# One level of Strassen-Winograd in the q/k/v projection of a dilated-attention layer, with the layout, buffers and evacuations that it needs

## The chip, the cores and the metric

The kernel runs on all 8 cores of one Trainium2 chip, one sequence of the batch on each core; nothing is exchanged between cores. The metric is the device time of the slowest core in microseconds (us). A program on 8 cores has a slower state here: the cores of one die (0 to 3 or 4 to 7), sometimes of both, get a lower TensorE clock in some executions.

## The reference, cut to what matters

A trunk of two layers: an mLSTM mixer, then a mixture of three dilated sliding-window attentions, each layer followed by a gated ConvFFN. The change touches the attention mixer:

```python
D_MODEL = 2048; BATCH = 8; SEQ = 2048
A_HEAD_DIM = 128; A_HEADS = 16
A_GROUPS = ((128, 1), (512, 4), (2048, 16))     # (window, dilation)

def dilated_mixer(h, positions, w_in, w_out):
    proj = (h @ w_in).astype(jnp.float32).reshape(B, S, A_N_GROUPS, 3, A_HEADS, A_HEAD_DIM)
    for g, (window, dilation) in enumerate(A_GROUPS):
        q = partial_rope(proj[:, :, g, 0], positions)      # rope on 32 of 128 channels
        k = partial_rope(proj[:, :, g, 1], positions)
        o, lse = dilated_band_attention(q, k, proj[:, :, g, 2], window, dilation)
        ...
    alpha = jax.nn.softmax(jnp.stack(lses), axis=0)
    o = jnp.sum(alpha[..., None] * jnp.stack(outs), axis=0)
    return o.reshape(B, S, A_WIDTH).astype(h.dtype) @ w_out
```

For a core this is, 48 times (16 heads x 3 groups), a product of 2048 tokens x 2048 features x 384 columns (128 each of q, k, v), a banded attention, and a sum over the three groups of numerators and denominators.

## The kernel before

Each engine has its own instruction stream. A recording layer tracks who wrote and read which 256-byte page of SBUF and which PSUM bank, and sets the semaphore waits. The attention stage walks over 768 units of 128 tokens. In a unit, TensorE makes the projection in one accumulation of 16 matmuls; the tokens are the stationary operand, the 384 weight columns the moving one:

```python
    def P(n):
        idx, u = divmod(n, 16)
        ...
        for kc in range(16):
            R.mm(PS[:, bk, 0:384], c.hT[:, kc, ts_], W[:, kc, :], kc == 0, kc == 15)
        R.act(QKV[:, n % 16, :], PS[:, bk, 0:384], AF.Copy)               # ScalarE
        R.copy("dve", Rr[(n // 4) % 2][:, n % 4], ...)                    # VectorE, rope channels
```

`ts_` takes every first, fourth or sixteenth token, by the group's dilation. Some units later follow, for four units at a time, rope on GpSimd (`rope`) and the transposes of q and k (`Tr`), and for pairs of units scores, exp and mask (`Sm`) and the products with v and with ones (`AV`). In the third group the pair is finished, with columns 16 apart:

```python
            vN, vD = v3(accN[:]), v3(accD[:])
            R.tt("dve", vD, p3(pD), vD, ALU.add)
            R.recip(vD, vD)                                               # VectorE
            R.tt("dve", vN, p3(pN), vN, ALU.add)
            R.tt("pool", v3(c.yT[:, h, :]), vN, vD, ALU.mult)             # GpSimd
```

Then the output projection (`phase_out`) multiplies `yT` by its weights. At the start of the stage the norm of the last quarter of the tokens (`c.pend`, made by `second`) is still under way and is worked off beside the first units.

The softmax here doesn't subtract the row's maximum and nothing guards it: scores larger than these inputs give would overflow.

Of the kernel before, what the change touches and what calls it, by code (L numbers as in the profile page):

```python
# [19 lines left out]
PAGE = 256  # L20
# [274 lines left out]
def unit_tokens(g):  # L295
    d = ATT_GROUPS[g][1]
    nb = S // d // 128
    tok = np.zeros((16, 128), dtype=np.int64)
    for r in range(d):
        for n in range(nb):  # L300
            tok[r * nb + n] = r + d * (128 * n + np.arange(128))
    return tok
# [75 lines left out]
def build_program():  # L378
# [10 lines left out]
    T["rope"] = nc.dram_tensor("rope", [128, 2, 768], F32, kind="Internal").ap()  # L389
    T["wdb"] = nc.dram_tensor("wdb", [2, 16, 4, 128, 11, 128], BF16, kind="Internal").ap()  # L390
# [32 lines left out]
    c.B = R.sb("B", [128, 7, 8, 512], F16, c.HA)  # L423
    c.yT = R.sb("yT", [128, 16, S], BF16, c.R1)
# [490 lines left out]
class out_weights:  # L915
# [9 lines left out]
    def load(self):  # L925
        if self.n < 16:
            self.c.R.dma("pool", self.w[self.n][:], self.c.T["m_wo" if self.l == 0 else "a_wo"][self.n], f"ow{self.n}")
            self.n += 1
# [17 lines left out]
def norm_tiles(c, li, src, tq, rstd, xr, xcnt, out_dram=None):  # L946
# [14 lines left out]
    for fc in range(ahead):  # L961
        ld(fc)
    for fc in range(16):
        if fc + ahead < 16:
            ld(fc + ahead)
        x = xr[(base + fc) % len(xr)]
        R.stt(x[:], x[:], gvec[:, fc:fc + 1], rstd, ALU.mult, ALU.mult)
        if shv is not None:
            up = li in (2, 3)
            R.act(quarter(c, tq, fc) if up else c.hT[:, fc, sl], x[:], AF.Identity, bias=shv[:, fc:fc + 1])  # L970
            if up and tq % 2 == 1 and fc >= 8:
                combine(c, fc - 8)
        else:
            c.final.append(R.dma("sp", T["outT"][:, fc, sl], x[:], f"st_o{(base + fc) % len(xr)}", dw=[("out", fc, tq)]))
        yield
    xcnt[0] = base + 16

def phase_out(c, l):
# [17 lines left out]
    while W.n < 16:  # L996
        W.load()
# [10 lines left out]
    for tb in range(2):  # L1008
        for fo in range(16):
            for sub in range(2):  # L1010
# [17 lines left out]
                m += 1  # L1028
                if tb == 1 and fo >= (1, 4)[l]:
                    bg = pull(bg, 1 + (m % (4, 2)[l] == 0))  # L1030
# [97 lines left out]
def phase_ffn(c, l):  # L1128
# [106 lines left out]
    for tb in range(2):  # L1235
# [17 lines left out]
        for n_, (fo, ss) in enumerate(order):  # L1253
# [30 lines left out]
            if tb == 1:  # L1284
                if fo == 15:
                    drain(bg)
                    s_ = ss[0]
                    bg = final_norm(c, acc[s_], rst, xk, s_) if last else second(c, li, dst, 2 + s_, acc[s_], rst, nx)
# [8 lines left out]
def second(c, li, src, tq, acc, rst, xr):  # L1297
    rstd_of(c, acc[:], rst[:], 7)
    yield
    yield from norm_tiles(c, li, src, tq, rst[:], xr, [0])  # L1300
# [14 lines left out]
def phase_attn(c):  # L1315
    R, T, PS = c.R, c.T, c.PS
    o = c.R2
    wa = c.att_w
    cur = [o]
    lim = [o + kb(24)]  # L1320

    def t(name, shape, dt_, n=1):
# [5 lines left out]
        for i in range(n):  # L1328
            if lim[0] < c.END and cur[0] + b > lim[0]:
                cur[0], lim[0] = o + kb(48), c.END  # L1330
            r.append(R.sb(f"a_{name}{i}", shape, dt_, cur[0]))
            cur[0] += b
        assert cur[0] <= lim[0], (name, cur[0], lim[0])
        return r if n > 1 else r[0]
    QKV = t("qkv", [128, 16, 384], BF16)
    qkT = t("qkT", [128, 2, 16, 128], BF16)
    PT = t("PT", [128, 4, 128], BF16, 2)
    Rr = t("R", [128, 4, 2, 32], F32, 2)
    cs = t("cs", [128, 2, 48, 16], F32)
    tA = t("tA", [128, 2, 4, 16], F32)  # L1340
    tB = t("tB", [128, 2, 4, 16], F32)
    t("pad", [128, 256], F32)
    accD = t("accD", [128, S], F32)
    accN = t("accN", [128, S], F32)
    mask = t("mask", [128, 4, 128], BF16)
    mrow = t("mrow", [128, 128], F32)
    bg = c.pend
    c.pend = None
    wab = [R.sb(f"a_wab{i}", [128, 16, 128], BF16, c.R1 + kb(56 + 4 * i)) for i in range(2)]
    LO, HI, EVERY, FIRST = 128, 192, 8, 20  # L1350

    def ada_load(i):
        if i < HI:
            R.dma("pool", wab[i % 2][:], T["w_ada"][i], f"wab{i % 2}")
    ada_load(LO)
    ada_load(LO + 1)
    R.dma("sp", cs[:].rearrange("p a b c -> p (a b c)"), T["rope"].rearrange("p a b -> p (a b)"), "ropel", dr=["rope"])
    for i in range(4):
        R.copy("pool", mask[:, i, :], c.tri[:] if i < 2 else c.tri_ge[:])
    seq = [(h, g) for h in range(16) for g in range(3)]  # L1360
    NU = len(seq) * 16

    def utok(g, u):
        d = ATT_GROUPS[g][1]
        nb = S // d // 128
        r, n = u // nb, u % nb
        st = r + d * 128 * n
        return slice(st, st + d * 127 + 1, d) if d > 1 else slice(st, st + 128)

    def P(n):  # L1370
        idx, u = divmod(n, 16)
        h, g = seq[idx]
        if u == 0 and idx + 1 < len(seq) and idx > 0:
            c.att_load(idx + 1)
        W = wa[idx % 2]
        bk = n % 2
        ts_ = utok(g, u)
        for kc in range(16):
            R.mm(PS[:, bk, 0:384], c.hT[:, kc, ts_], W[:, kc, :], kc == 0, kc == 15)
        ct, part = LO + (n - FIRST) // EVERY, (n - FIRST) % EVERY  # L1380
        here = n >= FIRST and ct < HI
        if here and part == 0:
            ada_rows(c, ct, wab[ct % 2], mrow, PS[:, bk, 384:512])
        if here and part == 1:
            ada_sum(c, ct, mrow, PS[:, bk, 384:385])
        R.act(QKV[:, n % 16, :], PS[:, bk, 0:384], AF.Copy)
        R.copy("dve", Rr[(n // 4) % 2][:, n % 4], PS[:, bk, 0:256].rearrange("p (a d) -> p a d", a=2)[:, :, 0:32])
        if here and part == 0:
            R.act(mrow[:], PS[:, bk, 384:512], AF.Copy)
            ada_load(ct + 2)  # L1390
        if here and part == 1:
            R.tt("dve", c.modT[:, ct:ct + 1], PS[:, bk, 384:385], c.badaT[:, ct:ct + 1], ALU.add)
            gm_after(c, ct)

    def rope(j):
        g = seq[j // 4][1]
        u0 = (j % 4) * 4
        s0 = (j % 4) * 4
# [4 lines left out]
        q = QKV[:, s0:s0 + 4, 0:256].rearrange("p u (a d) -> p a u d", a=2)  # L1403
# [7 lines left out]
    def Tr(j, qk):  # L1411
        s0 = (j % 4) * 4
        for i in range(4):
            R.mm(PS[:, 2 + qk, i * 128:(i + 1) * 128], QKV[:, s0 + i, qk * 128:(qk + 1) * 128], c.identb[:], True, True)
        out = qkT[:, qk, s0:s0 + 4, :]
        in_ = PS[:, 2 + qk, :].rearrange("p (u s) -> p u s", u=4)
        if qk == 0:
            R.copy("dve", out, in_)
        else:
            R.act(out, in_, AF.Copy)  # L1420

    def pair(m):
        idx, j = divmod(m, 8)
        h, g = seq[idx]
        nb = S // ATT_GROUPS[g][1] // 128
        a, b = 2 * j, 2 * j + 1
        return idx, j, h, g, a, b, a % nb > 0, b % nb > 0

    def Sm(m):
        idx, j, h, g, a, b, pa, pb = pair(m)  # L1430
        bk = 4 + m % 2
        sl = lambda u: u % 16
        R.mm(PS[:, bk, 0:128], qkT[:, 1, sl(a), :], qkT[:, 0, sl(a), :], True, True)
        R.mm(PS[:, bk, 128:256], qkT[:, 1, sl(b), :], qkT[:, 0, sl(b), :], True, True)
        n = 2
        if pb:
            R.mm(PS[:, bk, 256:384], qkT[:, 1, sl(b - 1), :], qkT[:, 0, sl(b), :], True, True)
            n = 3
        if pa:
            R.mm(PS[:, bk, 384:512], qkT[:, 1, sl(a - 1), :], qkT[:, 0, sl(a), :], True, True)  # L1440
            n = 4
        pt = PT[m % 2]
        R.act(pt[:, 0:n, :], PS[:, bk, 0:n * 128].rearrange("p (a s) -> p a s", a=n), AF.Exp, scale=128.0 ** -0.5)
        R.tt("dve", pt[:, 0:n, :], pt[:, 0:n, :], mask[:, 0:n, :], ALU.mult)

    def AV(m):
        idx, j, h, g, a, b, pa, pb = pair(m)
        bk = 6 + m % 2
        pt = PT[m % 2]
        V = lambda u: QKV[:, u % 16, 256:384]  # L1450
        R.mm(PS[:, bk, 0:128], V(a), pt[:, 0, :], True, not pa)
        if pa:
            R.mm(PS[:, bk, 0:128], V(a - 1), pt[:, 3, :], False, True)
        R.mm(PS[:, bk, 128:256], V(b), pt[:, 1, :], True, not pb)
        if pb:
            R.mm(PS[:, bk, 128:256], V(b - 1), pt[:, 2, :], False, True)
        if not pa:
            R.mm(PS[:, bk, 256:384], c.onesb[:], pt[:, 0, :], True, True)
            R.mm(PS[:, bk, 384:512], c.onesb[:], pt[:, 1, :], True, not pb)
            if pb:  # L1460
                R.mm(PS[:, bk, 384:512], c.onesb[:], pt[:, 2, :], False, True)
        else:
            R.mm(PS[:, bk, 256:384], c.onesb[:], pt[:, 0, :], True, False)
            R.mm(PS[:, bk, 256:384], c.onesb[:], pt[:, 3, :], False, True)
            R.mm(PS[:, bk, 384:512], c.onesb[:], pt[:, 1, :], True, False)
            R.mm(PS[:, bk, 384:512], c.onesb[:], pt[:, 2, :], False, True)
        pN, pD = PS[:, bk, 0:256], PS[:, bk, 256:512]
        if g == 0:
            R.copy("dve", accN[:, j * 256:(j + 1) * 256], pN)
            R.copy("dve", accD[:, j * 256:(j + 1) * 256], pD)  # L1470
        elif g == 1:
            st = j // 2 + 512 * ((j % 2) * 2)
            vN, vD = accN[:, st:st + 1021:4], accD[:, st:st + 1021:4]
            R.tt("dve", vN, pN, vN, ALU.add)
            R.tt("dve", vD, pD, vD, ALU.add)
        else:
            r0 = 2 * j
# [70 lines left out]
```

## Time and profile before

| | before |
|---|---|
| first four executions | 7414.49, 7443.39, 7601.44, 8290.82 us |
| profiled execution | 7443.39 us; cores 7396.2 to 7441.9 |
| attention stage, first to last projection matmul | 2367 us, a third of the whole |
| TensorE busy, granted clock in its body | 99%, 1.00 |

The profile is a page with the busy time of each engine, the chain of work that ended last, and groups of equal instructions ("line engine op out<-in shapes xcount | busy us, mean ns of one | idle time before them, and who ended it"). Rows of stretches give the busy time of TensorE, its weight loads, VectorE (DVE), ScalarE (ACT) and GpSimd (POOL) in a window, then granted clock, DMA share and GB/s. Rows in order of time give start, duration and instruction; for a run of matmuls the duration is that of the whole run. Matmuls are pipelined, so their cost is the distance of their starts, not their duration.

### The profile page before, as it was taken

Reading aid. Unit: us, or ns where it says so; the run is one execution under the profiler, and the core shown is the slowest. Engines: PE = TensorE matmul, PEld = TensorE weight load, DVE = VectorE, ACT = ScalarE, POOL = GpSimd, SP = SyncE. Lnnn points to the kernel's source line nnn. Section 1 sums busy time; section 2 is a strip of 40 time slices with the busy share of each in tenths; the row PEclk is TensorE's granted clock in tenths of the full one; section 3 lists DMA queues with packets and bytes.
Section 4 is the critical chain, followed back from the end, with each engine's and each line's share of the span. In section 5 each row is a group of like instructions: output and inputs, shape, how many; then the busy total and the mean of one; then the engine's idle time right before and its main releaser. Section 6 shows DMA issues by size and latency. Waiting matters only on the chain.

```text
span 7441.9 us, 123344 instructions; the slowest of 8 cores (7396.2 to 7441.9 us)
## 1 busy us (share of the span) xinstructions
PE 7072.9 (95%) x44216; PEld 4078.8 (55%) x44216; DVE 3694.1 (50%) x6832; ACT 2326.2 (31%) x4277; POOL 2203.9 (30%) x3196
## 2 busy tenths in 40 slices
PE   3799999999999999899999999999999999999998
PEld 2466664444444444477777777777754444444443
DVE  2443342688328872244444444444435885268822
ACT  2644442344214432222222222222213443134410
POOL 1422222333222333233333333333233222222232
PEclk9899998999999999999999999999999999999999
DMA  9157746766676658533333333211156444555566
GB/s 177 46 90 123 121 73 175 150 111 109 144 162 105 108 120 258 166 55 68 73 70 65 69 71 73 52 32 34 35 135 176 87 88 112 171 102 86 89 215 214
DMA packets 258971, 820.78 MB, mean 110 GB/s; under 512 B 32320, under 2 KB 33856, under 8 KB 250176
## 3 DMA queue, kind: packets, MB, share of 16 engines
q0 software_dynamic: 134672, 587.34, 42.1%
q1 hardware_dynamic: 123696, 225.54, 9.6%
q8 instruction: 361, 5.91, 0.3%
q14 instruction: 242, 1.98, 0.1%
HBM read 1206.30 MB, written 124.52 MB: 179 GB/s over the span
## 4 chain that ended last, share of the span: by engine, by line
PE 81%; DMA 5%; DVE 5%; issue 3%; POOL 3%; ACT 2%; SPq 1%; DVEq 0%; POOLq 0%; ACTq 0%
PE PS L211 81%; DMA f_d<-xb 2%; DMA outT<-f_d 1%; POOL yT L229 1%; DMA s_wa<-w_ada 1%; DVE a_accD L242 1%; POOL a_qkv L229 1%; SPq L205 1%; DVE f_tv L225 1%; POOL a_tB L229 0%; DVE f_tg L225 0%; DMA f_down<-wdb 0%; DVE a_accD L229 0%; POOL a_tA L229 0%; DMA o_y<-xa 0%
## 5 line engine op out<-in xcount | busy, mean ns | idle before, releaser
L211 PE MATMUL PS<-a_wa,hT 128*128 128x384 bf16 x12288 | 2095.4, 326 | 13.7 <-DVE a_R L239 13.7
L211 PEld LDWEIGHTS PS<-a_wa,hT 128*128 128x128 bf16 x12288 | 1421.2, 119 | 508.4 <-issue 18.1
L211 PE MATMUL PS<-B,f_up 128*128 128x512 f16 x5632 | 1303.9, 379 | 5.4 <-DVE PS L229 3.2
L211 PE MATMUL PS<-f_act,f_down 128*128 128x512 bf16 x5632 | 1228.3, 381 | 26.8 <-DMA f_down<-wdb 22.1
L211 PE MATMUL PS<-B,f_ws 128*128 128x512 f16 x4224 | 1004.6, 381 | 31.9 <-DVE f_ws L229 25.4
L211 PEld LDWEIGHTS PS<-f_act,f_down 128*128 128x128 bf16 x5632 | 552.4, 98 | 703.8 <-issue 49.3
L211 PEld LDWEIGHTS PS<-B,f_up 128*128 128x128 f16 x5632 | 550.9, 98 | 672.9 <-issue 12.3
L221 ACT ACTIVATE a_qkv<-PS 128x384 bf16<-128x384 f32 x768 | 376.3, 490 | 1656.4 <-PE PS L211 1656.4
L211 PEld LDWEIGHTS PS<-B,f_ws 128*128 128x128 f16 x4224 | 413.9, 98 | 537.1 <-issue 43.7
L239 DVE COPY a_R<-PS 128x64 f32<-128x64 f32 x768 | 172.4, 224 | 1059.1 <-ACT a_qkv L221 1056.9
L229 POOL TENSOR_TENSOR f_act<-f_tg,f_tv 128x1024 bf16<-128x1024 f32 x176 | 413.8, 2351 | 808.8 <-DVE f_tv L225 732.3
L211 PE MATMUL PS<-m_wkvo,hT 128*128 128x320 bf16 x4096 | 616.8, 303 | 0.0
L229 POOL TENSOR_TENSOR a_tA<-a_R,a_cs 128x128 f32<-128x128 f32 x384 | 175.1, 456 | 1107.0 <-DVE a_R L239 1079.2
L225 DVE SCALAR_TENSOR_TENSOR f_tg<-PS,f_cw,f_tg 128x1023 f32<-128x1023 f32 x352 | 450.7, 1280 | 91.9 <-ACT f_tg L221 72.4
L211 PEld LDWEIGHTS PS<-m_wkvo,hT 128*128 128x128 bf16 x4096 | 399.1, 100 | 150.3
L211 PE MATMUL PS<-yT,o_w 128*128 128x512 bf16 x2048 | 476.6, 399 | 5.0 <-POOL yT L229 5.0
L225 DVE SCALAR_TENSOR_TENSOR f_tv<-PS,f_cw,f_tv 128x1023 f32<-128x1023 f32 x352 | 450.9, 1281 | 54.9 <-ACT f_tv L221 29.2
L221 ACT ACTIVATE f_tg<-PS,f_cb,f_cw 128x1024 f32<-128x1024 f32 x176 | 211.9, 1204 | 752.9 <-DVE PS L229 752.9
L221 ACT ACTIVATE f_p<-PS 128x512 f32<-128x512 f32 x528 | 312.9, 594 | 329.8 <-PE PS L211 313.1
L205 POOL DMA_DIRECT2D f_up<-f_wu x352 | 194.7, 553 | 725.2 <-PE PS L211 719.4
L229 DVE TENSOR_TENSOR PS<-PS,f_p 128x512 f32<-128x512 f32 x528 | 350.6, 695 | 116.5 <-PE PS L211 115.8
L211 PEld LDWEIGHTS PS<-yT,o_w 128*128 128x128 bf16 x2048 | 208.2, 102 | 273.3 <-issue 108.2
(182 smaller groups left out, 7170.0 us busy)
## 6 DMA issues: line engine op xcount, KB each, us to landing
f_up<-f_wu POOLq DMA_DIRECT2D x352, 512.0 KB, 6.2
f_down<-wdb POOLq DMA_DIRECT2D x320, 352.0 KB, 4.5
a_wa<-a_wi POOLq DMA_DIRECT2D x48, 1536.0 KB, 10.8
f_d<-xa SPq DMA_DIRECT2D x192, 256.0 KB, 5.0
wdb<-f_wd POOLq DMA_DIRECT2D x128, 352.0 KB, 5.7
m_wab<-w_ada POOLq DMA_DIRECT2D x64, 512.0 KB, 6.5
xa<-o_n SPq DMA_DIRECT2D x128, 256.0 KB, 3.7
a_wab<-w_ada POOLq DMA_DIRECT2D x64, 512.0 KB, 6.5
```

Source lines behind the costliest of these rows:

```text
L205: self.q[eng].append((ws, lambda e, o=out, i=in_: e.dma_start(out=o, in_=i), sem))
L211: return self.op("pe", lambda e: e.matmul(out, lhsT=lhsT, rhs=rhs, start=start, stop=stop, **kw), [out], [lhsT, rhs])
L221: return self.op("act", lambda e: e.activation(**kw), outs, ins)
L225: return self.op("dve", lambda e: e.scalar_tensor_tensor(out=out, in0=in0, scalar=scalar, in1=in1, op0=op0, op1=op1), [out], ins)
L229: return self.op(eng, lambda e: e.tensor_tensor(out=out, in0=in0, in1=in1, op=op), [out], [in0, in1])
L239: return self.op(eng, lambda e: e.tensor_copy(out=out, in_=in_), [out], [in_])
L242: return self.op("dve", lambda e: e.reciprocal(out=out, in_=in_), [out], [in_])
```

## The change

Its intent is to make the projection with seven block products instead of eight. Even and odd tokens are the two row blocks, the halves of the 2048 features the inner blocks, and the halves of the 384 columns the column blocks. The token sums (T1 to T4) are made once for all heads, the weight sums (`WS`) once for each head and group. The intermediate results are added partly in PSUM (a product with `start` false adds to what its bank holds) and partly on the way out of it. The core of the diff:

```diff
-PAGE = 256
+PAGE = 128
+    c.BA = R.sb("BA", [128, 7, 8, 1024], F16, c.HA)       # 4 blocks of tokens, 3 more for sums
...
+    def w_sum(i, W, eng="pool"):                            # four sums of weight blocks
+        o, x, y, op = ((WS[:, 0], a21, a22, ALU.add), (WS[:, 1], WS[:, 0], a11, ALU.subtract),
+                       (WS[:, 2], a12, WS[:, 1], ALU.subtract), (a21, a11, a21, ALU.subtract))[i]
+    def mm8(bank, quart, ts_, w, start):
+        for k in range(8):
+            R.mm(PS[:, bank, 0:192], BA[:, quart, k, ts_], w[:, k, :], ...)
...
+            mm8(ka, B11, ts_, part(W, 0, 0), True)
+            R.act(s1[:], PS[:, ka, 0:192], AF.Copy)
+            Tr(n - 3)
+            mm8(kb_, T1, ts_, WS[:, 0], True)
+            R.act(s5[n % 2][:], PS[:, kb_, 0:192], AF.Copy)
+            mm8(KC, B21, ts_, part(W, 0, 1), True)
+            R.tt("dve", QK[:, q0, 0:192], PS[:, KC, 0:192], s1[:], ALU.add)
+            Sm(n - 3)
+            mm8(ka, T2, ts_, WS[:, 1], False)
+            R.act(s16[:], PS[:, ka, 0:192], AF.Copy)
+            mm8(KA[(n - 1) % 2], T4, ..., part(wa[i1 % 2], 1, 1), False)     # of the pair before
+            AV(n - 4)
+            mm8(kb_, B22, ts_, WS[:, 2], False)
+            R.tt("dve", QK[:, q0 + 1, 0:192], ps, s16[:], ALU.add)
+            mm8(ka, T3, ts_, part(W, 1, 0), False)
+            R.tt("dve", dest(n)[:, 1, :], ps[:, 64:192], s5[n % 2][:, 64:192], ALU.add)
...
-            R.recip(vD, vD)
+            R.act(vD, vD, AF.Ln)
+            R.act(vD, vD, AF.Exp, scale=-1.0)
...
+                R.dma("sp", T["yat"][h], Y, "yat", dw=[("yat", h)])          # y of a head to DRAM
...
+            c.y_first = [y_back(0, h0) for h0 in (0, 5, 10)]                 # and back at the end
...
-    bg = ... second(c, li, dst, 2 + s_, acc[s_], rst, nx)
+    bg = ... second(c, li, dst, 2 + s_, acc[s_], rst, nx + xn + acc[0:1] if s_ else nx)
```

So beside the products it changes the order of the tokens, the type of the operands (f16), the place of y (its room is taken by the blocks), the reciprocal, the depth of the ring of x tiles in the last norm, and the page size of the tracking. Outside this cut it also gives all transposed copies to ScalarE, loads the weights of a head and group in four pieces instead of one, and puts v of the first group in order by small transfers.

## The prediction

> **What bounds the kernel now.** I read the page first (shares of engines, the chain that ended last), then the groups of instructions, then the attention stage alone by stretches and in order of time. The page:
>
> ```profile
> PE 7072.9 (95%) x44216; PEld 4078.8 (55%) x44216; DVE 3694.1 (50%) x6832; ACT 2326.2 (31%) x4277; POOL 2203.9 (30%) x3196
> PE 81%; DMA 5%; DVE 5%; issue 3%; POOL 3%; ACT 2%; SPq 1%; DVEq 0%; POOLq 0%; ACTq 0%
> ```
>
> TensorE is busy 95% of the span and is 81% of the chain; no other engine is above 50%. The change touches the attention stage, whose largest part is the costliest group of all, the projection to q, k and v (first the page's row, then that tile's own view, then three stretches of the stage):
>
> ```profile
> L211 PE MATMUL PS<-a_wa,hT 128*128 128x384 bf16 x12288 | 2095.4, 326 | 13.7 <-DVE a_R L239 13.7
> ...
> L211 PE MATMUL PS<-a_wa,hT x12288: 322/326/524, 3083.2 to 5450.3; 128*128 128x384 bf16 x199
> ...
> 3083.00:3170.00 87.00, 69.03 (x484) 43.29 (x483) 27.52 (x61) 28.36 (x53) 18.96 (x40) 0.92 0.48 111
> 3170.00:5433.00 2263.00, 2246.19 (x17940) 1692.54 (x17938) 995.84 (x2220) 618.58 (x1359) 736.91 (x1400) 1.00 0.30 57
> 5433.00:5477.00 44.00, 26.55 (x178) 19.94 (x177) 26.93 (x41) 6.77 (x17) 17.15 (x25) 0.84 0.28 60
> ```
>
> (Stretch rows: busy PE, weight loads, DVE, ACT, POOL, then granted clock, DMA share, GB/s.) The stage runs from 3083 to 5450, 2367 us, a third of the program. In its body TensorE idles 17 of 2263 us at full clock; DVE is at 44%, ACT at 27%. So here time falls only if TensorE gets fewer or shorter matmuls. The two ends are looser: 18 us idle at the start, 17 at the end.
>
> "Mean 326 ns" is not the cost of a matmul, since they are pipelined. The order of time gives the cost:
>
> ```profile
> 4499.95 0.39 PE L211 MATMUL PS<-g_identb,a_qkv 128*128 128x128 bf16 x4
> 4500.17 0.39 PE L211 MATMUL PS<-a_qkT 128*128 128x128 bf16 x4
> 4500.40 0.39 PE L211 MATMUL PS<-a_PT,a_qkv 128*128 128x128 bf16 x4
> 4500.62 0.39 PE L211 MATMUL PS<-a_PT,g_onesb 128*128 128x128 bf16 x4
> 4500.84 5.36 PE L211 MATMUL PS<-a_wa,hT 128*128 128x384 bf16 x32
> ```
>
> Four matmuls of 128 columns start every 0.22 us: 56 ns each. Thirty-two of 384 columns take 5.36 us, less the 0.33 us of one, over 31: 162.5 ns each. Both lie on N/2.4 ns plus 2.5 to 2.7.
>
> **What the Trainium skill says.** "TensorE: Matmul & The Clock Gate", section "Back-to-back issue gap", gives N/2.4 + 2.5 ns warm, which the trace confirms, but also some 81 ns as sustained pace for N=128 with a weight load before each; this trace has 56, so the measurement decides. The same page, section "LDWEIGHTS (loading the stationary operand)", has a load's time follow from its columns alone; the trace shows that it also depends on the stride of the tokens. These rows are stretches inside a group of dilation 1, 4 and 16:
>
> ```profile
> L211 PEld LDWEIGHTS PS<-a_wa,hT 128*128 128x128 bf16 x88 | 8.5, 98 | 5.3
> ...
> L211 PEld LDWEIGHTS PS<-a_wa,hT 128*128 128x128 bf16 x82 | 9.0, 113 | 3.5
> ...
> L211 PEld LDWEIGHTS PS<-a_wa,hT 128*128 128x128 bf16 x136 | 19.0, 144 | 2.3
> ```
>
> The same page's Part 1 warns of a 13/16 clock when three cores of a die run dense matmuls; the attention body here has 1.00, so it is not tripped there. "ScalarE: Activation LUTs", section "Table sets: the hidden batching unit", has one set with both ln and exp: no reload between them. The trace agrees: the last reload before attention is at 2803 us, ahead of a norm's ln, and the exps of attention come after without another.
>
> **The change, part by part.** (1) The projection (2048 tokens x 2048 x 384 for each of 48 head-groups) becomes one level of Strassen-Winograd: even and odd tokens, halves of the contraction, halves of the columns. Eight block products become seven. Per pair of token tiles 32 matmuls of 384 columns become 56 of 192. There are 384 pairs. Before: 12288 x 162.6 ns = 1998 us. After: 21504 at 192/2.4 + 2.6 = 82.6 ns = 1776 us. This removes **222 us** and doubles the weight loads. Strassen's ideal eighth would be 250; 28 are lost to the fixed 2.6 ns on 9216 more matmuls.
>
> (2) The small matmuls (1536 transposes, 3 x 1200 of attention; 5136 x 56 ns = 288 us) are as many as before, and so is the modulation work (some 32 us). So TensorE needs about 2318 us before, and the measured 2367 contain 49 of waits: about 19 at the start, the rest spread (the largest named is the transposes waiting for POOL's rope, 17 us). After it needs 2096.
>
> (3) VectorE gets the post-additions. From 695 ns for 128x512 out of PSUM and 224 for 128x64 I take 1.05 ns a column: 358 ns for 192, 291 for 128. Per pair 2 x 358 + 3 x 224 + 291 = 1.68 us, x 384 = 645 us. Weight sums: four per head-group over 1536 f16; 1024 take 0.69 to 0.71 us, so 1.05 each, 202 us. Gone: reciprocal 225, rope copies 172, one of the transpose copies 132. Net +318: 1040 becomes about 1360 of 2140 us, 64%. Not a bound on average. In the eighth pair of a group three weight sums fall together: about 3.6 + 3.2 us in a 5.4 us iteration. The surplus of some 1.4 us runs into the next pair, where every consumer has about that much slack.
>
> (4) ScalarE: 277 ns for 128 columns and 594 for 512 give 0.83 ns a column. Per pair 3 x 330 + 224 + 277 + 594 = 2.1 us, 801 in all, instead of 376 + 114; ln and exp in place of the reciprocal, 256 x 0.39 = 99. Total about 1050 of 2140 us, 49%. POOL as before with 144 more weight issues of 0.59 us, hidden.
>
> (5) Start: token sums (three of about 0.7 us on DVE a tile) beside the rest of the norm. DVE has 3.0 + 2.1 + 3.1 us in each of the first seven iterations against 5.4 of TensorE: about 20 us of waiting, plus 4 for the first sums. Deeper prefetch takes away the wait for x of before. Net **+5**.
>
> (6) End: the blocks cover part of the output's place, so each head's y goes to DRAM; 15 heads' halves (3.9 MB) come back before the output projection. At about 200 GB/s (that stage moved 211) some 20 us, alongside the drain of the last five pairs, which took 26 us before. Net **+5**. The second 3.9 MB ride through a projection whose DMA engines were 84% busy: **+5**.
>
> (7) Waits in the body: 384 iterations with about nine cross-engine waits each. The transposes get a whole iteration for rope, so most of the old 17 us goes; single-buffered PSUM banks and the DVE surplus bring others. Net **+12**, with the largest uncertainty.
>
> Sum: -222 + 5 + 5 + 5 + 12 = **-195 us**.
>
> **Rivals.** *A: weight loads become the bound.* A load takes 98 to 144 ns and now comes every 83. For: at a stride of 16 a load lasts longer than that. Against: at 128 columns loads of 98 ns sustain a start every 56, so they are pipelined; strides also fall from 1, 4, 16 to 1, 2, 8 units. If only the group with stride 8 were paced at 98 ns: 7168 x 15 = +110 us, gain 85, within 2%. *B: VectorE or ScalarE sets the pace.* For: 64% and 49% on average, in-order queues, and single buffers. Against: every link I laid out by hand (product, evacuation, next accumulation) has 0.2 us or more to spare. If each pair lost 0.4 us: +150, within 2%. *C: the clock trips to 13/16 in the denser stream.* Against: the f16 feed-forward runs at 1.00. It would add 2096 x (16/13 - 1), some 480 us: slower. *D: the slow ends grow* (y's round trip not overlapped): +20 to +40, gain still about 155.
>
> **Range and chances.** The two undisturbed runs before are 7414.49 and 7443.39, mean 7429; less 195 is 7234. A median may contain a run in the slower state, so I say **7245 us**, 8 in 10 between **7165** and **7360**. Two per cent is 149 us; my gain is 195 with about 60 for A, B and D, so 0.74 faster, 0.22 within 2%, 0.04 slower (C, or B in full).
>
> **What would show it.** In the changed profile: the projection's matmuls as 21504 of 128x192 at starts 82 to 83 ns apart, also in the stride-8 group (above 90: A). TensorE idle in the body under 40 us; if over 100 and ended by DVE or ACT: B, and the rows name the operation. DVE near 64% and ACT near 49% there. No table reload between ln and exp. Granted clock 1.00. The first seven pairs about 8 us each, later ones 5.4. A gap of 20 to 30 us ahead of the output projection, ended by the y transfers. The prediction is wrong if the stage is not 2367 - 185 = about 2180 us to within 50.

## The result, and the profile after

| | before | after |
|---|---|---|
| median of all executions | 7577.74 us (18 runs) | 7232.25 us (11 runs) |
| fast executions | 7414.49 to 7469.63 (8) | 7202.7 to 7232.25 (6) |
| ratio of the fast runs | | 0.9697, 95% interval 0.9675 to 0.9719 |
| profiled execution, slowest core | 7441.9 us | 7200.8 us |

A ratio is the mean time of one kernel's fast runs over that of the other's of the same rounds (here 7215.9 over 7441.3), so not quite the ratio of the medians. On a later chip, whose runs of before were less disturbed, the same two kernels had 7196.53 and 7197.73 against 7408.52, 7415.08 and 7417.62: 0.971.

The page of the changed kernel has these lines for engines and chain:

```profile
PE 6821.8 (95%) x53242; PEld 4416.7 (61%) x53432; DVE 4034.9 (56%) x8264; ACT 2814.4 (39%) x5877; POOL 2357.0 (33%) x3348
PE 85%; DMA 5%; DVE 3%; issue 2%; ACT 2%; POOL 1%; SPq 1%; DVEq 0%; ACTq 0%; POOLq 0%
```

TensorE still sets the time. The two projection groups, then the stage in stretches (start, body, end, first half of the output projection):

```profile
L211 PE MATMUL PS<-a_wa,BA 128*128 128x192 f16 x12288 | 1209.0, 247 | 12.4 <-ACT a_s L221 7.5
...
L211 PE MATMUL PS<-a_ws,BA 128*128 128x192 f16 x9216 | 957.1, 247 | 7.5 <-DVE BA L229 4.0
```

```profile
3051.00:3127.00 76.00, 56.73 (x531) 51.43 (x530) 58.98 (x107) 29.80 (x69) 38.12 (x37) 0.80 0.41 104
3127.00:5200.00 2073.00, 2054.06 (x27075) 2030.37 (x27073) 1312.55 (x3613) 1093.46 (x2921) 873.19 (x1557) 1.00 0.40 73
5200.00:5227.00 27.00, 17.35 (x199) 15.81 (x197) 13.03 (x33) 16.30 (x36) 12.33 (x18) 0.83 0.53 185
5227.00:5340.00 113.00, 109.35 (x488) 48.91 (x496) 23.86 (x33) 20.24 (x32) 43.69 (x43) 0.98 0.93 234
```

The stage now runs from 3051 to 5215: 2164 us against 2367 on the slowest core, 2160 to 2165 against 2367 to 2371 over all cores. In its body VectorE is at 63% (1312.55 of 2073), ScalarE at 53%, and TensorE idles 19 us. The order of time has the cost of a matmul:

```profile
4501.95 0.82 PE L211 MATMUL PS<-a_ws,BA 128*128 128x192 f16 x8
4502.61 0.82 PE L211 MATMUL PS<-a_wa,BA 128*128 128x192 f16 x8
```

Eight matmuls start every 0.66 us, 82.5 ns each. Their weight loads, in a stretch of a second and one of a third group, where the stationary operand takes every second and every eighth token:

```profile
L211 PEld LDWEIGHTS PS<-a_wa,BA 128*128 128x128 f16 x187 | 15.7, 98 | 0.0
...
L211 PEld LDWEIGHTS PS<-a_wa,BA 128*128 128x128 f16 x172 | 15.2, 144 | 0.0
```

A load of 144 ns does not keep the starts apart: over the third groups their mean distance is 83.0 ns, over the first two 82.5.

**Where the 241 us between the two profiled executions come from.** The stage gives 204. The way from its last product to the output projection is 11 instead of 16 us, and the output projection no longer waits 5 us for the last y. Some 28 us are not the change's: in the profiled execution of before, six of the eight cores had a 13/16 clock for about 160 us in the first output projection (which took 253 instead of 225 us). The pages show it in their clock rows, before and after:

```profile
PEclk9899998999999999999999999999999999999999
```

```profile
PEclk9899999999999999999999999999999999999999
```

The two cores of before without that dip (2 and 3) spent 7410 and 7396 us, the cores after 7179 to 7201: 211 us in the mean.

### The profile page after: what moved, and what is told of

Its sections match the earlier page's. It is cut to its first block, busy times and chain, and to the rows that moved or that the text cites. A ratio compares the mean times of both kernels' runs of the same rounds, so it can differ in the third digit from the quotient of the medians.

```text
span 7200.8 us, 152147 instructions; the slowest of 8 cores (7179.0 to 7200.8 us)
## 1 busy us (share of the span) xinstructions
PE 6821.8 (95%) x53242; PEld 4416.7 (61%) x53432; DVE 4034.9 (56%) x8264; ACT 2814.4 (39%) x5877; POOL 2357.0 (33%) x3348
## 4 chain that ended last, share of the span: by engine, by line
PE 85%; DMA 5%; DVE 3%; issue 2%; ACT 2%; POOL 1%; SPq 1%; DVEq 0%; ACTq 0%; POOLq 0%
PE PS L211 85%; DMA outT<-f_d 2%; DMA s_wa<-w_ada 1%; DMA o_x<-xb 1%; SPq L205 1%; DVE f_tv L225 0%; POOL yT L229 0%; DMA o_h<-xa 0%; DMA s_xB<-xT 0%; DVE f_tg L225 0%; ACT a_accD L221 0%; POOL a_tB L229 0%; DMA f_down<-wdb 0%; DMA f_d<-xb 0%; DMA s_posi<-posu 0%
## 5 line engine op out<-in xcount | busy, mean ns | idle before, releaser
L211 PE MATMUL PS<-a_wa,BA 128*128 128x192 f16 x12288 | 1209.0, 247 | 12.4 <-ACT a_s L221 7.5
L211 PEld LDWEIGHTS PS<-a_wa,BA 128*128 128x128 f16 x12288 | 1052.9, 114 | 17.6 <-issue 16.4
L211 PE MATMUL PS<-a_ws,BA 128*128 128x192 f16 x9216 | 957.1, 247 | 7.5 <-DVE BA L229 4.0
L211 PEld LDWEIGHTS PS<-a_ws,BA 128*128 128x128 f16 x9216 | 772.9, 114 | 8.9 <-issue 8.4
L229 POOL TENSOR_TENSOR f_act<-f_tg,f_tv 128x1024 bf16<-128x1024 f32 x176 | 413.8, 2351 | 806.2 <-DVE f_tv L225 758.8
L221 ACT ACTIVATE a_s<-PS 128x192 f32<-128x192 f32 x1152 | 379.6, 330 | 569.5 <-PE PS L211 289.1
L229 DVE TENSOR_TENSOR a_qk<-PS,a_s 128x192 bf16<-128x192 f32 (+1 forms) x1152 | 354.3, 308 | 383.7 <-PE PS L211 283.5
L229 POOL TENSOR_TENSOR a_tA<-a_R,a_cs 128x128 f32<-128x128 f32 x384 | 202.6, 528 | 811.9 <-DVE a_qk L229 543.2
L211 PE MATMUL PS<-yT,o_w 128*128 128x512 bf16 x2006 | 445.4, 382 | 5.7 <-DVE o_n L225 2.3
```

What stands on the lines that cost most here:

```text
L211: return self.op("pe", lambda e: e.matmul(out, lhsT=lhsT, rhs=rhs, start=start, stop=stop, **kw), [out], [lhsT, rhs])
L221: return self.op("act", lambda e: e.activation(**kw), outs, ins)
L229: return self.op(eng, lambda e: e.tensor_tensor(out=out, in0=in0, in1=in1, op=op), [out], [in0, in1])
```

## The experiments

All outputs are right. "Groups" are the median times from one head-group to the next, over all cores and all groups at full clock. For the first, second and third dilation they are 49.1, 49.6 and 48.6 us before, and 45.4, 44.5 and 43.6 after; these medians shift by some tenths of a us with the matmul at which a group is cut off. The first group of the stage, with the norm beside it, is told apart: about 68 us before, 75 after. "Waits of TensorE" are the distances of starts beyond N/2.4 + 2.6 ns, summed over the stage from the trace (excesses under some 25 ns left out): 67 us before and 84 after, on core 4.

### 1. Eight products in the new schedule (e1_eight_wide)

This undoes the seven products alone. Layout, f16, order of work, ring of x, ln and exp, and y through DRAM stay.

```diff
-            mm8(ka, B11, ts_, part(W, 0, 0), True)   # ... seven products, sums, additions
+        for k in range(8 * hf, 8 * hf + 8):           # even tokens, then odd ones
+            R.mm(PS[:, bank, 0:384], BA[:, (0, 1, 2, 3)[2 * r + k // 8], k % 8, ts_], W[:, k, :], k == 0, k == 15)
+        R.act(QK[:, q0 + r, :], ps[:, 0:256], AF.Copy); R.act(dest(n)[:, r, :], ps[:, 256:384], AF.Copy)
```

> The new schedule, layout, f16, prefetch, ln/exp and y round trip are kept; only the seven products with their sums are replaced by the plain eight, as 32 matmuls of 384 columns a pair. Theory (the number of columns streamed by TensorE sets the stage): 32 x 162.5 ns + 748 ns = 5.95 us a pair instead of 5.37, so the stage is 2164 + 222 = about 2386 us less the start's sums (some 10), and the whole about 0.998 of before (0.990 to 1.005). Rival (layout and schedule bring most of the gain): whole below 0.985 of before. VectorE share in the stage falls back to about 40%.

Correct. The chip of this job was throttled throughout: before had 7751.74 to 7814.24 us in its quicker runs, this kernel 7757.67 to 7820.06, so the whole is about equal to before, without a verdict. The stage tells more. On cores 6 and 7, with 15 us of low clock, it took 2346 and 2349 us (expected 2386), groups 48.5, 49.1 and 48.4. Its body on core 7:

```profile
3240.00:5480.00 2240.00, 2237.92 (x17864) 1618.27 (x17862) 714.16 (x1908) 1020.60 (x2516) 799.05 (x1534) 1.00 0.36 67
```

TensorE idles 2 us of 2240, and VectorE is at 32% (expected 40%). My figure of 2386 was too high: I had added the eighth product to the stage after, whose waits come with the sums and go with them. So the seven products are worth about 2347 - 2164 = 183 us, nine tenths of the gain, and everything else together 20 us. The rival (layout and schedule bring most) falls.

### 2. Eight narrow products (e2_eight_narrow)

As experiment 1, but in two halves of 192 columns, as wide as Strassen's: 64 matmuls and weight loads a pair instead of 32.

```diff
+        for k in range(16):
+            R.mm(PS[:, bank, 192 * hf:192 * hf + 192], BA[...], W[:, k, 192 * hf:192 * hf + 192], k == 0, k == 15)
```

> As the eight wide products, but as 64 matmuls of 192 columns a pair, with twice the weight loads. Theory (192 columns cost 82.6 ns and a load is hidden): 64 x 82.6 = 5.29 us against 5.20, stage 32 us longer than with wide ones, and one product more than the changed kernel: 8 x 82.6 x 384 = 254 us above its stage, about 2405 us; whole about 1.003 of before. Rival (weight loads of 144 ns at stride 8 pace narrow matmuls): over 80 us longer than with wide ones, the starts in the third kind of group above 90 ns.

Stage 2379 and 2376 us on cores 6 and 7 (24 to 28 us of low clock), 30 us above the wide ones (expected 32). VectorE and ScalarE do the same in both, so the price of narrow matmuls is the fixed 2.6 ns and nothing more. The rival, that loads of 144 ns pace them, falls: a group of the third kind took 49.1 us against 48.4, no more than the others. Against this kernel the seven products save about 214 of the ideal 254 us (one in eight of 64 x 82.6 ns x 384 pairs). The other 40 are the waits that the sums bring: by the same distances TensorE waits 41 us in this stage (core 7), against 84 in the changed kernel. The absolute figure of 2405 us was too high for the same reason as in experiment 1.

### 3. The reciprocal back on VectorE (e3_recip)

```diff
-            R.act(vD, vD, AF.Ln)
-            R.act(vD, vD, AF.Exp, scale=-1.0)
+            R.recip(vD, vD)
```

> The changed kernel with the reciprocal on VectorE again instead of ln and exp on ScalarE. If VectorE has room (theory, it is at 63%): the third kind of group has 3.3 + 1.76 + 0.5 us of VectorE in 5.2 us of TensorE a pair, so it becomes just bound there: +20 to +60 us, 0.973 to 0.978 of before. If VectorE never matters (only the columns do): unchanged, 0.970. If VectorE is already the bound of that group: +1.76 us x 128 = +225 us, 1.00.

Groups at full clock: 48.1, 44.7 and 44.4 us (45.4, 44.5 and 43.6 with ln and exp), so about 16 x 3.7 = 59 us more in the stage, at the upper edge of what the first theory expected. TensorE in the body on core 5 now waits for VectorE's additions (first and third row), which no row of the changed kernel's body names:

```profile
PE PS L211 <- DVE a_v L229: 39.2, 16, 3.2
PE PS L211 <- POOL a_qk L229: 8.3, 29, 0.6
PE PS L211 <- DVE a_vs L229: 3.2, 6, 0.8
```

"a_v" is VectorE's last addition of a pair, which frees the bank for the next product. It comes 16 times, once a head, 15 of them in the first pair after a third group, where the last reciprocals of that group and the weight sums of its eighth pair meet on VectorE. So most of the loss lies in the groups of the first kind (45.4 to 48.1 us) and not of the third, where I had looked for it. An engine at 63% on average has no room there.

### 4. Ln and exp alone in the kernel before (e5_before_lnexp)

```diff
-            R.recip(vD, vD)
+            R.act(vD, vD, AF.Ln)
+            R.act(vD, vD, AF.Exp, scale=-1.0)
```

> The kernel before with ln and exp on ScalarE instead of the reciprocal, this part of the change alone. Theory: VectorE at 44% is off the path before, so nothing changes: 0.997 to 1.003 of before. Rival (part of the gain comes from relieving VectorE): 0.99 or less.

Against my theory. The stage takes 2342 to 2344.5 us on all cores (10 to 14 us of low clock) instead of 2367 to 2371. The medians of the groups of the first kind fall from 49.1 to 48.2 us, the others stay; summed group by group, 21 us go in the first kind, 3 in the third and 1 in the first group of all. In the kernel before this line stands for the body's waits of TensorE:

```profile
PE PS L211 <- POOL a_qkv L229: 16.7, 39, 1.0
```

With ln and exp the same view has no line at all. By distance of starts, the waits ahead of the transposes in groups of the first kind fall from 23 to 2 us. So 25 us of the whole change could be had by these two lines. That VectorE was "at 44%" and ended few waits by name did not mean that its reciprocal (1.76 us at a time) cost nothing: the wait bore the name of the rope. The kept traces show the link in order of time. One wait of 0.39 us in the kernel before, in a group whose first product starts at 3687.00 (core 4):

```profile
3686.41 1.76 DVE L242 RECIPROCAL a_accD<-a_accD 128x256 f32<-128x256 f32 x1
3688.08 0.54 DVE L229 TENSOR_TENSOR a_accN<-PS,a_accN 128x256 f32<-128x256 f32 x1
...
3688.77 1.29 POOL L229 TENSOR_TENSOR yT<-a_accN,a_accD 128x256 bf16<-128x256 f32 x1 [4.51 <-DVE a_R L239]
...
3689.78 0.46 POOL L229 TENSOR_TENSOR a_tA<-a_R,a_cs 128x128 f32<-128x128 f32 x1
...
3692.49 0.45 POOL L229 TENSOR_TENSOR a_qkv<-a_tA,a_tB 128x128 bf16<-128x128 f32 x1
...
3693.09 0.38 PE L211 MATMUL PS<-g_identb,a_qkv 128*128 128x128 bf16 x4 [0.39 <-POOL a_qkv L229]
```

The numerator's sum stands behind the reciprocal on VectorE, GpSimd's multiplication waits for that sum, the rope stands behind the multiplication, and the transposes wait for the rope. Over the 120 groups of the first kind after the third, counted from each one's first product, the multiplication starts at 1.76 us (median) and the rope ends at 5.94. With ln and exp it is 1.00 and 5.14, and the transposes, at 5.54, no longer wait.

### 5. The start without GpSimd's sum (e4_start)

```diff
-        ... ("pool", T3, B22, B12), ...
+        ... ("dve", T3, B22, B12), ...
-        R.copy("pool", mask[:, i, :], ...)
+        R.act(mask[:, i, :], ..., AF.Copy)
```

> The changed kernel with the one token sum that GpSimd makes moved to VectorE, and the mask copies moved from GpSimd to ScalarE, so that GpSimd leaves VectorE alone in the first eight pairs. Read from the stage at full clock, not from the time. Theory (VectorE operations with two operands in SBUF last as long as the GpSimd operation beside them: 0.7 us became 2.0 to 2.6): some 11 us of stretching go, 6 us of sums come, so the first group of eight pairs takes 70 instead of 75.5 us. Rival (the start waits for x or for ScalarE alone): 75 us or, with VectorE loaded more, 80.

7192.41 us in its fast run. The first group takes 67.9 to 72.2 us, median 70.0, instead of 71.8 to 76.5, median 75.0: as expected. VectorE's token sums, first with one sum in four on GpSimd, then with all on VectorE (first group of the stage):

```profile
L229 DVE TENSOR_TENSOR BA<-BA 128x1024 f16<-128x1024 f16 x24 | 20.5, 856 | 0.8 <-DVE BA L229 0.2
L225 DVE SCALAR_TENSOR_TENSOR f_d<-f_d,g_gm,f_d 128x512 f32<-128x512 f32 x16 | 16.4, 1027 | 3.5 <-DMA f_d<-xb 3.5
```

```profile
L229 DVE TENSOR_TENSOR BA<-BA 128x1024 f16<-128x1024 f16 x32 | 22.7, 714 | 0.8 <-DVE BA L229 0.2
L225 DVE SCALAR_TENSOR_TENSOR f_d<-f_d,g_gm,f_d 128x512 f32<-128x512 f32 x16 | 12.2, 764 | 3.9 <-DMA f_d<-xb 3.9
```

Thirty-two sums now take 22.7 us where 24 took 20.5, and the norm's operations fall from 1027 to 764 ns. So some 8 us of stretching went, not 11. VectorE's busy time in the group fell by only 3.6 us (58.1 to 54.5); that the moved sum is itself ready sooner (0.7 us on VectorE, 2.5 on GpSimd) may have its part in the 5 us, and this run does not separate the two. In the order of time a sum of 0.69 us had lasted 2.60 beside GpSimd's 2.27 us one:

```profile
3055.43 2.60 DVE L229 TENSOR_TENSOR BA<-BA 128x1024 f16<-128x1024 f16 x1
...
3055.21 2.27 POOL L229 TENSOR_TENSOR BA<-BA 128x1024 f16<-128x1024 f16 x1
```

This agrees with the Trainium skill, "GPSIMD Engine Reference", section "Specifications": GpSimd's interfaces to SBUF are shared with VectorE, with contention where a VectorE instruction has two inputs in SBUF. VectorE's additions of 192 columns out of PSUM, with one input in SBUF, took 352 ns alone and 356 beside GpSimd.

### 6. The weight sums twice (e6_sums_twice)

Three of the four sums of each group are repeated; the result is the same.

```diff
+        for _ in range(1 if i == 3 else 2):
             R.tt(eng if i == 3 else "dve", o, x, y, op)
```

> The changed kernel with three of the four weight sums of each group computed twice: 3 us more of VectorE in the eighth pair of each group, 144 us in all. Read from the groups at full clock (45.3, 44.5, 43.6 us now). As the reciprocal showed, VectorE has little room: each group 1.5 to 3 us longer, 70 to 144 us in all. Rival (slack of the following pairs takes it up): under 0.5 us a group.

7383.59 us. Second and third groups take 2.3 and 2.6 us longer; the stage 2347 to 2351, 184 to 188 more, for only some 140 us of VectorE work. The rest is the clock: all cores had 174 to 191 us of low clock in the stage (14 to 31 in the changed kernel), and every group of the first kind had some. TensorE's waits in the body (core 4):

```profile
PE PS L211 <- DVE a_v L229: 60.1, 31, 3.3
PE PS L211 <- ACT a_qkT L221: 36.5, 15, 3.0
PE PS L211 <- DVE a_vs L229: 33.3, 15, 2.8
```

The slack of the following pairs takes up next to nothing. And a wait of 2 to 3 us costs more than itself, as TensorE then runs at half clock for some microseconds: the body on core 4 has 34 stretches at clock 0.50, of 3.4 or 6.8 us each, and every one has a wait of 1.9 to 3.3 us beside it. The Trainium skill, "TensorE: Matmul & The Clock Gate", Part 1, describes this clock gate, but has the half clock follow an idle window of about 3.4 us; here shorter waits were enough.

### 7. The short ring of x (e8_short_ring)

```diff
-            second(c, li, dst, 2 + s_, acc[s_], rst, nx + xn + acc[0:1] if s_ else nx)
+            second(c, li, dst, 2 + s_, acc[s_], rst, nx)
```

> The changed kernel without the deeper ring of x tiles in the norm of the last quarter (two buffers again as before). If this part of the change matters, the wait for x of the kernel before comes back in the first group: 8 to 15 us longer than 75.5. Rival (the start is paced by VectorE and ScalarE): under 3 us longer.

The first group takes 87.2 to 90.5 us instead of 71.8 to 76.5, the stage 2176 to 2180. As expected, the wait for x is back (3.5 us in the changed kernel, as the rows of experiment 5 show):

```profile
DVE f_d L225 <- DMA f_d<-xb: 22.2, 6, 8.5
```

So this part keeps about 14 us of loss away from a start that is loaded more heavily than before.

### 8. The multiplication behind the rope (e9_both)

The start of experiment 5, and y's multiplication on GpSimd recorded after the rope of the same pair.

```diff
-            R.tt("pool", v3(Y), vN, vD, ALU.mult)
+            def mult(): ...            # returned by AV, called after rope(n // 2) in odd pairs
```

> Meant to beat both kernels: the start of the other run here, and the multiplication that makes y on GpSimd set behind the rope of the same pair, where it stands before it now. Theory: the transposes at the start of each first-kind group wait 0.9 us for a rope that stands behind a 1.4 to 1.7 us multiplication; this goes, 13 us in all, the first-kind groups 45.3 to 44.5; with the start some 20 us, 0.3% of the whole, 0.967 of before. Rival (the rope is late because VectorE is, and the multiplication only fills the gap): groups unchanged.

Slower than the changed kernel (7196.53 to 7232.25 us on its chips): 7262.74 and 7267.97 us in its fast runs. The first group is 70 us again, but first and third groups became 47.6 and 45.0 us, the stage 2223 to 2236. The rope's wait is gone from TensorE's list. In its place stands another (TensorE's first line, then VectorE's line that is new):

```profile
PE PS L211 <- ACT a_qkT L221: 66.9, 54, 2.6
```

```profile
DVE a_accD L229 <- POOL yT L229: 72.2, 36, 2.4
```

VectorE's next sum of denominators waits for the late multiplication. Their columns are different ones, but interleaved 16 apart, so they share pages in the tracking. ScalarE's ln stands behind that sum, and the transposed copy behind ln.

### 9. Contiguous sums (e10_contig), the changed kernel beside it (e11_after), and the late multiplication again (e12_contig_later)

The start of experiment 5; in the third group the two sums go to small contiguous tiles instead of back into the interleaved accumulators.

```diff
+    tD = t("tD", [128, 2, 128], F32, 2); tN = t("tN", [128, 2, 128], F32)
+        oD, oN = (tD[n % 2][:], tN[:]) if g == 2 else (vD, vN)
-        R.tt("dve", vD, p3(pD), vD, ALU.add)
+        R.tt("dve", oD, p3(pD), vD, ALU.add)          # then ln, exp, sum and product on oD, oN
```

> Meant to beat both kernels: the start of the run that moved the token sum, and in the third kind of group the sums of numerator and denominator go to small contiguous tiles instead of back into every sixteenth column, so that ln and exp on ScalarE should fall from 0.70 us each to the 0.39 us that 256 contiguous columns take in the exp of the scores, and the multiplication on GpSimd gets shorter and no longer shares tracked pages with the next pair's sum. Theory: the waits for the transposed copy (ScalarE, about 19 us over the first and third kind) and for the rope (GpSimd, 14 us) get smaller: groups 45.3 to 44.6 and 43.6 to 43.3, stage 2159 to about 2140, whole about 0.3 to 0.5% below the changed kernel of the same job. Rival: waits are set by VectorE's backlog of the eighth pair: groups unchanged.

> The changed kernel itself, unaltered, on the chip of this job, to compare the improved one with and to see the ratio where the kernel before isn't disturbed. Expected 0.970 of before (0.968 to 0.973), stage 2163 us.

> The contiguous sums, and besides the multiplication set behind the rope, which alone had made the stage 61 us longer. Theory: that loss came from the next pair's sum waiting for the late multiplication on shared pages (VectorE waited 72 us for it); with separate tiles the loss is gone, groups of the first kind within 0.5 us of the contiguous run and the rope wait under 5 us. Rival (the late multiplication hurts by itself, through the single numerator tile): still over 1.5 us a group longer.

On one chip: before 7408.52, 7415.08 and 7417.62 us; changed kernel 7196.53 and 7197.73; contiguous sums 7179.62, 7181.13 and 7182.19, which is 0.9686 of before (interval 0.9664 to 0.9708) and about 0.2% below the changed kernel (expected 0.3 to 0.5%). 0.2% is no more than executions of one kernel differ by; what shows the gain is the stage, 2143 to 2153 us on the eight cores (expected 2140) against 2159 to 2167. Ln and exp, first in the changed kernel's body, then with contiguous tiles:

```profile
L221 ACT ACTIVATE a_accD<-a_accD 128x256 f32<-128x256 f32 x244 | 170.9, 700 | 82.6 <-DVE a_accD L229 70.8 <-ACT a_accD L221 0.4
```

```profile
L221 ACT ACTIVATE a_tD<-a_tD x248: 416/417/424, 3192.3 to 5198.5; 128x256 f32<-128x256 f32 x124
```

The same 256 columns take 0.70 us with a step of 16 and 0.42 without. First-kind groups fall from 45.4 to 44.2 us, the rope's 14.5 us of waits on core 4 vanish; the third kind, where I had expected 0.3 us, stays at 43.5. With contiguous sums the late multiplication is harmless: 44.5, 44.5 and 43.5 us, 7178.79 us in its fast run. So the loss in experiment 8 did not come from the lateness itself, but from what stood behind it there. VectorE still waits for the late multiplication, 54.3 us on core 4 (72.2 there), but now with the numerator's sum, behind which no ln stands. (Ln and exp are also shorter here; these runs do not part the two.) The gain that I had hoped of the lateness is not there either.

## Why the prediction was right, point by point

Predicted were 7245 us and 195 us of gain; the fast runs of after have a mean of 7215.9, a ratio of 0.9697, and some 216 us of gain where neither kernel is disturbed (7413.7 against 7197.1, means of the later chip's runs).

1. **Seven products, -222 us.** Right. The distances are 82.5 ns and 83.0 with a stride of 8, so 21504 cost 1778 us instead of 1776. Experiment 2 has 12288 narrow matmuls more than experiment 1 and took 30 us longer, 2.4 ns each. The step's explanation of its 28 us is slightly off: 9216 times 2.6 ns are 24, and the other 4 are an eighth of the fixed cost before, which the "ideal" 250 counts as saved.
2. **Small matmuls as before.** Right in count. But "the rest spread" of the waits, with the rope as its largest name, hid the reciprocal (experiment 4): in the old schedule ln and exp end them.
3. **VectorE at 64%.** Measured 63%. The surplus of the eighth pair is there, but not the slack that I gave it: three more microseconds came back almost in full (experiment 6).
4. **ScalarE at 49%.** Measured 53%. The mis-sized term is ln and exp: 256 x 0.70 instead of 256 x 0.39 us, 179 instead of 99. I had taken the duration of a contiguous exp for a step of 16. No table load fell in the stage, as expected.
5. **Start +5.** The cause was right in the main, the size too small: 75 instead of 68 us, which with a group's own 49 and 45 makes about +11. The first five pairs took 9.7 to 13.7 us, not 8, in part because of GpSimd's sum (experiment 5: 5 us). That VectorE is the bound there is read from names, in two steps: of TensorE's 19.3 us of waits on core 0, 15.3 bear ScalarE's name, and ScalarE's norm operations in turn waited 22.6 us for VectorE's.
6. **End +5 and +5.** This step failed: the end gained about 10 us. In the drain (the work left after the last product) the core's DMA moved 270 to 410 GB/s and not my 200; the three loads of y landed in 7 to 10 us each, the last about a microsecond before the output projection began. So there was no gap of 20 to 30 us. The drain itself is shorter (11 instead of 16 us), and the wait for the last y fell from 5 us to about one. The second half of y did not slow the projection, which took 225 to 229 us, against 230 to 232 before.
7. **Waits in the body +12.** By distance of starts they went from 43 to 52 us outside the first group: +9. The net was right, its make-up only in part. Ahead of the transposes, where the rope is waited for, 31 us became 15; the new schedule ends this wait only without the sums (0.1 us in experiment 1). Ahead of the scores 7 us became 24, of which 6 bear the name of ScalarE's transposed copy. And the +12 took no account of the reciprocal: with it on VectorE the same schedule loses some 59 us more (experiment 3). That the net came out so near is partly luck.

For the stage the steps gave -222 + 5 + 12 = -205, and -204 was measured (-222 + 11 + 9 by the terms above). The total came out about 20 us better than predicted, which is step 6 alone. The sentence at the prediction's end, with "2367 - 185 = about 2180", contradicts its own steps by 20 us; the stage lay within the margin given there. Of the rivals, A fell by the distances and by experiment 2. B was right in kind at one place, around the eighth pair of the third group, but small: in the body on core 4 the waits named there are 12.1 us for GpSimd's rope and 5.7 for ScalarE's copy. C did not happen in the profiled fast execution: the attention body had a clock of 1.00. D went the other way.

What stays open: the 20 us that all other parts gave together. Ln and exp alone give 25 in the old schedule, so that layout, y's round trip and the new order would cost about 5; but the parts don't simply add, as ln and exp are worth 59 us in the changed kernel. The smaller page size, f16 and the order of the tokens were not tried alone.

## What to carry to other kernels

When an engine is at 99% at full clock, count what it streams: an eighth of the columns less cut the streaming by what the arithmetic said (222 us), of which the waits of the sums left 183; and the fixed cost of narrower instructions could be read off in advance from two widths in the same trace. Look for the room of the other engines where work comes together, not on average: an engine at 44% or 63% can still hold up the bound one once in each period, and the wait may bear another engine's name. Before moving an operation to another engine, take its duration at the stride that it will really have.

## What the Trainium skill lacked or had wrong

- "TensorE: Matmul & The Clock Gate", section "LDWEIGHTS (loading the stationary operand)", has the load's time depend on the columns alone. Here 128 columns took 98 ns at element steps of 1 and 2, 113 at a step of 4, and 144 at 8 and at 16 (two-byte types). "SBUF — State Buffer", in the note on 16-byte lines within the section "Door 1: The DMA port swizzle", fits from a step of 8 on, where each element lies in another line; but at a step of 4, with two elements in a line, which the note counts as full bandwidth, the load already took 113 instead of 98. That loads run ahead of matmuls the TensorE page does say, in its first table; that a load may last longer than the distance of the starts (144 against 83 ns) and still stay hidden, only the runs show.
- The same TensorE page, section "Back-to-back issue gap", gives about 81 ns as sustained pace for N=128 with weight loads, and about 131 for N=512. Here bursts of N=128 started every 56 ns, and N=512 every 216 (median, feed-forward and output projection of the kernel before); the page's N/2.4 + 2.5 held for N of 128, 192, 384 and 512.
- The same page, Part 1, says to budget 13/16 of the clock for dense matmuls on all cores. Here eight cores with TensorE at 99% had 1.00 through the attention body in the profiled fast executions; what the page describes is what the slow runs show, with means of 0.81 to 0.84 over a whole run on one die in the worst of them. Its idle window of about 3.4 us ahead of the half clock was longer than the 1.9 to 3.3 us that were enough in experiment 6.
- "ScalarE: Activation LUTs", which this document used for table sets, has no figure for strided operands: ln and exp over 256 columns of f32 in SBUF took 0.70 us at a step of 16 and 0.42 contiguous.
